# PSUM banks by name: a turn of eight outside a recurrent scan, a list of 258 inside it

## The chip, the cores and the metric

The kernel runs on one core of a Trainium2 chip. Five engines work side by side on their own queues: TensorE (PE, matmuls), VectorE (DVE), ScalarE (ACT), GpSimd (POOL), and SyncE (SP), which here issues the DMAs. Matmuls write to PSUM, an on-chip memory of eight banks of 128 partitions by 2 KB; the other engines read the results from there. The metric is the device time of one execution in microseconds, the median of the runs shown.

## What is computed

One layer of a hybrid diffusion block over 512 latent tokens and 256 context tokens of width 1024: a combined input projection feeds an RWKV-7 branch (token shift, a delta-rule scan in two directions over 16 heads of 64) and a gMLP branch; gates merge them, an output projection follows, and then an expert-choice mixture of 16 SwiGLU experts. Cut to what matters for the stages that the change touches:

```python
def centred_shift(z, w):
    zp = jnp.pad(z, ((0, 0), (1, 1), (0, 0)))
    return zp[:, :-2] * w[0] + zp[:, 1:-1] * w[1] + zp[:, 2:] * w[2]

def decay(dw, w0, w2):                                  # rwkv_prep, per direction
    w = -jax.nn.softplus(-(w0 + jnp.tanh(dw) @ w2)) - 0.5
    return jnp.exp(-jnp.exp(heads(w)))
a_f = jax.nn.sigmoid(p["a0"][0] + daf @ p["a2"][0])
kk = kk * lax.rsqrt(jnp.maximum(jnp.sum(kk * kk, -1, keepdims=True), 1e-12))

def step(S, inp):                                       # rwkv_scan
    r_t, k_t, v_t, d_t, kk_t, a_t = inp
    s_kk = jnp.einsum('bhvk,bhk->bhv', S, kk_t)
    S_new = (S * d_t[:, :, None, :] - s_kk[..., None] * (kk_t * a_t)[:, :, None, :]
             + v_t[..., None] * k_t[:, :, None, :])
    y = jnp.einsum('bhvk,bhk->bhv', S if reverse else S_new, r_t)
    return S_new, y

def token_mixer(h, p, s0_f, s0_b, n_chunks):
    z = h @ p["w_in"]
    ...
    merged = g_a * (y_a @ p["w_branch_a"]) + g_s * (y_s @ p["w_branch_b"])
    return merged @ p["w_out"], s_f, s_b
```

## The kernel before

The stages follow one another along the span: loads, the modulation and the transposed inputs (`ht`) up to about 60 us; the projection with its preparation of the scan in eight blocks of 128 channels up to about 330; the gMLP values `zv`, gates and spatial gating up to 575, with the first parts of the scan mixed in; the scan's chunk steps from 575 to 862; readout, branches and output projection up to about 1000; and the experts to the end.

Every matmul group writes one PSUM tile of 128 by 512 float32, a full bank. All 789 of them come from one call, `P` (L70), which takes them from a pool with a single tag and eight buffers (L54); the framework decides which buffer a tile gets when the one it takes is free again by its own model of the work. The program puts a semaphore wait in front of a tile's first matmul for the last reader of the tile that had the bank before. PE, ACT and SP run in the order in which the program is written (`manual_schedule`, L56); DVE and POOL too in the block loop and in the scan, where the code is again under `manual_schedule`.

In the block loop (L575 on), block `ct` does in written order: `z_k` (matmuls `zl` and `zc` over the latent and the context tokens), `prep_d1(ct-1)` (the reverse direction of the block before, nearly all of it on DVE), the shift of k (`shift_in`, L344: one ACT pass at L352, two DVE passes each for `zc` and `zl`, L354 and L356, into `kt`), `prep_v(ct-1)` (twelve transposes into four `vT` tiles, PE L513, read by ACT at L514), `prep_bonus(ct-1)` (`bon`), `prep_a(ct, 0)` (tiles `b2`, `b1`, `b1`; named `b` in the profile; the first matmuls go to the first `b1`), `prep_tanh` (four ACT passes, L427 and L428), the square of `kt` (ACT L402), `prep_scan` (DVE L436 and L438, ACT L440 to L445), `prep_kd` (DVE L449), `z_r` (`zl` and its shift into `rt`), `prep_k` (matmuls `b<-sq,bones`), work on DVE up to `prep_L`, then `z_v` and `prep_a(ct, 1)`. A block takes 18 PSUM tiles.

The scan runs 12 chunk steps of 64 tokens in two directions. Its order is a hand-written list of short words, `PLAN` (L1087) and `PLAN_END` (L1099), run by `run_plan` (L1115, called at L1376 to L1378): `K` transposes keys (`keys_t` L849, `bk`), `z`, `y`, `s` and `q` are the matmuls `zp`, `up`, `sp` and `qs` with what reads them (`zed` L862, `you` L871, `state` L880, `query` L897), `w` is the output `yp` (`why` L909), `a` the small products of a chunk (`prep` L679), `o` stores them for the triangular solve (`wave_out` L698, SP L704), `v`, `p`, `F` and `D` run the solve on DVE (`wave` L721, whose load of `Dt` is L723; rank-1 steps `tmpi` and `Xt` at L717 and L719), `i` loads its result (`wave_in` L744), and `V`, `X`, `S`, `U`, `R` and `l` are smaller steps and loads. So on each queue the order is fixed, and one late step holds what stands behind it.

Of the kernel before, what the change touches and what calls it, by code (L numbers as in the profile page):

```python
# [1 line left out]

# [5 lines left out]
F32 = mybir.dt.float32  # L8
# [35 lines left out]
def block_kernel(es: ExitStack, tc, x, ctx, cT, ada_w, ada_b, pc, rows, w_ch, w_vs, w2, a2, g2, sgu_w,  # L44
# [9 lines left out]
    pp = es.enter_context(tc.tile_pool(name="ps", bufs=8, space=PSUM))  # L54
# [5 lines left out]
    def nm(p):  # L60
        cnt[0] += 1
        return f"{p}{cnt[0]}"

    def T(shape, name="t", dt=F32):
        return big.tile(shape, dt, name=nm(name), tag="big", bufs=NBIG)

    def K(shape, name="t", dt=F32):
        return keep.tile(shape, dt, name=nm(name), tag="keep", bufs=NKEEP)

    def P(name="p"):  # L70
        return pp.tile([128, 512], F32, name=nm(name), tag="ps")

    def mm(o, l, r, start=True, stop=True):
        PE.matmul(o, l, r, start=start, stop=stop, skip_group_check=True)  # L74
# [144 lines left out]
    def ada_chunk(ws):  # L219
        p = P("ada")  # L220
        for k in range(KT):
            g = k % 4
            mm(p[32 * g:32 * g + 32, :], sP[:, k, :], ws[k // 2][:, k % 2, :], start=(k < 4), stop=(k >= 4))
        a = T([128, 512], "adao")
        S.activation(a, p, AF.Copy)
        return a
# [9 lines left out]
    def ada_cols(n):  # L236
        a = ada_chunk(aw.pop(n))
        p = P("adt")
        for b in range(4):
            PE.transpose(p[:, b * 128:b * 128 + 128], a[:, b * 128:b * 128 + 128], ident)  # L240
        which, b0 = divmod(n * 4, 8)
        dst = md[:, which, b0:b0 + 4, :]
        V.tensor_reduce(dst, p.rearrange("p (b g m) -> p b m g", b=4, g=4)[:, :, 0:2, :], AX.X, OP.add)
        V.tensor_tensor(dst, dst, adab_col[:, which, b0:b0 + 4, None].to_broadcast([128, 4, 2]), OP.add)
        if which == 1:
            V.tensor_scalar(dst, dst, 1.0, None, op0=OP.add)
# [23 lines left out]
    for d in range(2):  # L270
        for lst, src, nme in ((w2p, w2, "w2p"), (a2p, a2, "a2p")):
            t = T([128, D], nme)
# [7 lines left out]
    def hl(k):  # L280
        return hL[0][k // 2][:, k % 2, :], hL[1][k // 2][:, k % 2, :]

    def hc(k):
        return hC[0][k // 4][:, k % 4, :], hC[1][k // 4][:, k % 4, :]
# [23 lines left out]
    for k in range(KT):  # L308
        if k % 4 == 0:
            ada_cols(k // 4)  # L310
            ada_cols(k // 4 + 2)
            if k:
                zw.step()
        for (dst, i0, n, j) in ((hl(k), 2, 4, 0), (hc(k), 0, 2, 1)):
            p = P("ht")
            w = n * 128
            for i in range(n):
                PE.transpose(p[:, i * 128:i * 128 + 128], xts[i0 + i][:, k * 128:k * 128 + 128], ident)
            t = T([128, TL], "hf")
            V.tensor_scalar(t[:, :w], p[:, :w], md[:, 1, k, j:j + 1], md[:, 0, k, j:j + 1], op0=OP.mult, op1=OP.add)  # L320
            S.activation(dst[0], t[:, :w], AF.Copy)
            G.tensor_tensor(dst[1], t[:, :w], dst[0].bitcast(F32), OP.subtract)  # L322

    def zmm(w, want_ctx):
        wh, wl = (t.rearrange("p (k n) -> p k n", k=KT) for t in w)
        pl = P("zl")
        pc_ = P("zc") if want_ctx else None
        for k in range(KT):
            st, sp = k == 0, k == KT - 1
            hh, hlo = hl(k)  # L330
            mm(pl, wh[:, k, :], hh, st, False)
            mm(pl, wh[:, k, :], hlo, False, False)
            if want_ctx:
                ch_, cl = hc(k)
                mm(pc_[:, :TC], wh[:, k, :], ch_, st, False)
                mm(pc_[:, :TC], wh[:, k, :], cl, False, False)
                mm(pc_[:, :TC], wl[:, k, :], ch_, False, sp)
            mm(pl, wl[:, k, :], hh, False, sp)
        return pl, pc_
# [540 lines left out]
    def state(si, d):  # L880
        bk, sv, uv, svn = BK.pop((si, d)), SV[si, d], UV[si, d], SV[si + 1, d]
        u = uidx(si, d)
        sp = P("sp").rearrange("p (c n) -> p c n", c=KT)
        idt = (si, d) in IDENT
        if idt:
# [197 lines left out]
    for d in range(2):  # L1083
# [16 lines left out]
        "q10.1 p1 s9.1 U11 s9.0 w9 V10 h10.0 z10.1 X10 z10.0 p1 y10.1 h10.1 y10.0 p5 s10.1 R11 s10.0 p4 w10 p2 "  # L1100
        "i11 p1 z11.0 h10.2 p1 V11 p1 q11.1 X11 z11.1 h11.0 y11.0 q11.0 p3 y11.1 p2 h11.1 w11 h11.2 "
    ).split()
    IDENT = {(1, 0), (4, 0), (4, 1), (7, 1), (8, 0), (8, 1), (9, 1), (10, 1)}

    def finish_wave(w):
# [9 lines left out]
    def run_plan(plan, hook=None):  # L1115
        for t in plan:
            args = [int(a) for a in t[1:].split(".") if a]
            if t[0] == "h":
                hook(*args)
            elif t[0] == "t":  # L1120
                static_pair(1)
            else:
                OPS[t[0]](*args)
# [40 lines left out]
    def readout(half):  # L1164
        H = [K([128, 4, 256], "yAH", F32R) for _ in range(2)]
        L = [K([128, 4, 256], "yAL", F32R) for _ in range(2)]
        YA[half] = (H, L)
        for o, i in enumerate(HALF[half]):
            bo = GB[half][0][o]
            for b in range(2):  # L1170
                p = P("yT").rearrange("p (a n) -> p a n", a=4)
                pg = P("gg").rearrange("p (a n) -> p a n", a=4)
                t = T([128, 4, 128], "yf")
                for q in range(4):
                    ct = 4 * b + q
                    PE.transpose(p[:, q, :], yt[i][:, ct * 128:ct * 128 + 128], ident)
                    mm(pg[:, q, :], st_tp["g2"][:, ct * 128:ct * 128 + 128], sdg[:, i * 128:i * 128 + 128])
                for q in range(4):
                    ct = 4 * b + q
                    if b == 0:  # L1180
                        V.scalar_tensor_tensor(t[:, q, :], p[:, q, :], col("lnx_g", ct), bo[:, ct, :], op0=OP.mult, op1=OP.add)
                    else:
                        S.activation(t[:, q, :], p[:, q, :], AF.Copy, scale=col("lnx_g", ct))
                if b:
                    G.tensor_tensor(t, t, bo[:, 4 * b:4 * b + 4, :], OP.add)
                V.tensor_mul(t, t, pg)
                hd, ld = H[b][:, :, o * 128:o * 128 + 128], L[b][:, :, o * 128:o * 128 + 128]
                S.activation(hd, t, AF.Copy)
                V.tensor_tensor(ld, t, hd.bitcast(F32), OP.subtract)
# [43 lines left out]
    def out_mm(half, outs, mg, last=False):  # L1233
        ps = {(o, n): P("yx") for o in outs for n in range(2)}

        def term(q, k, w, ns):
            for o in outs:
                l = tuple(m[k // 4][:, k % 4, o * 128:o * 128 + 128] for m in mg)
                for n in ns:
                    cs = slice(n * 512, n * 512 + 512)  # L1240
                    mm3(ps[o, n], l, (w[0][:, cs], w[1][:, cs]), q == 0, q == KT - 1)

        for q, k in enumerate(range(KT) if half == 0 else KORD):
            if half == 0:
                w = aws.get(KT + k)
                if k in KRES:
                    wos[k] = w
            elif k in wos:
                w = wos[k]
                aws.fill()  # L1250
            else:
                w = wos[k] = aws.get(3 * KT - len(JRES) + KORD.index(k) - len(KRES))
            term(q, k, w, (0,) if last else (0, 1))
        if last:
            for q, k in enumerate(KORD):
                term(q, k, wos[k], (1,))
        return ps
# [101 lines left out]
    def early(si, at):  # L1359
# [8 lines left out]
        if si == nst - 1:  # L1368
# [4 lines left out]
            if at == 1:  # L1373
                readout(0)

    with tc.manual_schedule():  # L1376
        run_plan(PLAN)
    run_plan(PLAN_END, early)  # L1378
# [25 lines left out]
    ps = out_mm(0, (0, 1), MG.pop(0))  # L1404
# [7 lines left out]
    ps = out_mm(1, (0,), mg)  # L1412
    sid1 = out_ln(1, (0,), ps)
    next(sid1), next(sid1)
    ps = out_mm(1, (1,), mg, True)
# [36 lines left out]
    p = P("sT")  # L1452
# [233 lines left out]
```

## Time and profile before

| | us |
|---|---|
| median of 3 runs | 1976.82 (1973.1 to 1978.05) |
| the profiled execution | 1979.77 |
| its span, first to last instruction | 1978.0 |
| PE busy in the span | 1762.2 (89%) |
| DVE busy | 919.3 (46%) |
| ACT busy | 604.2 (31%) |
| mean granted TensorE clock | 0.967 of full speed |

The shares are means over stages with different limits, so they are to be read by stage: PE and DVE share the block loop, PE alone fills the stretch before the scan, chains of waits between PE, DVE and SP make the scan, and the experts' weights arriving by DMA set the pace at the end. Start times in the rows are microseconds from the span's start; a bracket at the end of a row is the time that the engine had been idle before it and what ended that.

### The profile page before, as it was taken

The numbers are of one execution on the slowest core, as the hardware profiler recorded it, in microseconds if no ns is written. First come the engines' busy times: TensorE is split into PE (matmuls) and PEld (weight loads), VectorE is DVE, ScalarE is ACT, GpSimd is POOL, SyncE is SP. The second block draws the span as 40 slices with busy tenths as digits, with TensorE's granted clock in tenths as the row PEclk, the third lists the DMA queues.
The fourth block names the chain that finished last, engine by engine and source line by source line (L and its number), as shares of the span: only waits on it lengthen the run. The fifth ranks groups of instructions, "written<-read, shape, count | busy, mean of one in ns | idle before, by whom it ended". The sixth has DMA issues, their size and how long they took to land.

```text
span 1978.0 us, 32483 instructions
## 1 busy us (share of the span) xinstructions
PE 1762.2 (89%) x13252; PEld 1122.8 (57%) x13252; DVE 919.3 (46%) x1685; ACT 604.2 (31%) x1058; POOL 239.2 (12%) x203
## 2 busy tenths in 40 slices
PE   6989999999987978788959999899998989899895
PEld 3877777878876867687844434334343323334324
DVE  6688886687837768786950020110102002020105
ACT  2666766233246645343221111101011101111101
POOL 4422234110110100055300000000000000000000
PEclk9999999999999989898969999999999999999998
DMA  9265657667697667584189999999999999999995
GB/s 331 92 194 155 188 155 238 193 225 228 237 261 160 154 146 179 114 266 138 65 348 427 426 428 426 426 427 427 426 427 427 427 427 426 427 427 427 427 418 201
DMA packets 363757, 590.34 MB, mean 298 GB/s; under 512 B 220372, under 2 KB 282324, under 8 KB 315480
## 3 DMA queue, kind: packets, MB, share of 16 engines
q1 hardware_dynamic: 363608, 588.26, 80.6%
q8 instruction: 105, 1.72, 0.3%
q14 instruction: 44, 0.36, 0.1%
HBM read 539.69 MB, written 47.71 MB: 297 GB/s over the span
## 4 chain that ended last, share of the span: by engine, by line
DMA 44%; PE 26%; DVE 11%; issue 3%; SPq 2%; ACT 1%; POOL 0%; DVEq 0%; ACTq 0%; POOLq 0%
DMA we<-in_e 42%; PE zl L74 5%; PE hh L74 3%; PE zv L74 2%; PE sc L74 2%; DVE tmpi L717 2%; PE bb L74 2%; DVE Xt L719 2%; PE yx L74 2%; PE qs L74 2%; PE yp L74 1%; PE sp L74 1%; PE zp L74 1%; PE l L74 1%; PE up L74 1%
## 5 line engine op out<-in xcount | busy, mean ns | idle before, releaser
L74 PE MATMUL hh<-we,xe 128*64 128x512 f32 x2048 | 463.1, 597 | 24.5 <-DMA we<-in_e 24.2
L74 PEld LDWEIGHTS hh<-we,xe 128*64 128x64 f32 x2048 | 148.9, 137 | 324.6 <-issue 267.1
L74 PE MATMUL ye<-we,hidT 128*64 128x512 f32 (+1 forms) x1216 | 254.7, 533 | 37.8 <-DMA we<-in_e 37.5
L1521 DVE TENSOR_TENSOR hd<-hd,hh 64x512 f32<-64x512 f32 x64 | 44.1, 690 | 519.1 <-ACT hd L1520 518.7
L74 PE MATMUL zl<-hL,H 128*128 128x512 f32 x816 | 259.6, 400 | 1.9 <-DVE hf L320 1.2
L74 PEld LDWEIGHTS ye<-we,hidT 128*64 128x64 f32 x1216 | 83.3, 136 | 201.3 <-DMA we<-in_e 106.0
L1520 ACT ACTIVATE hd<-hh 64x512 f32<-64x512 f32 x64 | 37.9, 592 | 491.6 <-PE hh L74 491.6
L74 PEld LDWEIGHTS zl<-hL,H 128*128 128x128 f32 x816 | 153.9, 191 | 30.6 <-issue 2.6
L160 POOL TENSOR_TENSOR L<-w,H 128x1024 fp32r<-128x1024 f32 x54 | 138.4, 2571 | 236.6 <-ACT H L159 197.5
L74 PE MATMUL zl<-hL,L 128*128 128x512 f32 x408 | 162.1, 397 | 2.5 <-DVE L L160 2.5
L1614 POOL TENSOR_TENSOR x<-x,row 128x1024 f32<-128x1024 f32 x2 | 4.6, 2340 | 989.3 <-DVE rv L129 989.3
L159 ACT ACTIVATE H<-w 128x1024 fp32r<-128x1024 f32 x91 | 95.0, 1054 | 88.5 <-DMA w<-in_w_ch 36.1
L1539 ACT ACTIVATE ye<-ye 64x512 f32<-64x512 f32 (+1 forms) x34 | 18.9, 555 | 272.8 <-PE ye L74 272.5
L1540 DVE SCALAR_TENSOR_TENSOR ye<-ye,gate,srow 64x512 f32<-64x512 f32 (+1 forms) x38 | 23.9, 663 | 149.1 <-ACT ye L1539 148.8
L74 PEld LDWEIGHTS zl<-hL,L 128*128 128x128 f32 x408 | 78.1, 191 | 14.4 <-DVE L L160 3.6
L717 DVE TENSOR_TENSOR tmpi<-Dt,Xt 128x31 f32<-128x31 f32 (+15 forms) x186 | 63.6, 342 | 18.0 <-DMA Dt<-Asd 12.5
L719 DVE TENSOR_TENSOR Xt<-Xt,tmpi 128x31 f32<-128x31 f32 (+15 forms) x186 | 63.8, 343 | 6.4
L74 PEld LDWEIGHTS xe<-oh,h 128*128 128x128 f32 x512 | 59.6, 196 | 8.9 <-issue 8.9
L74 PE MATMUL co<-ye,ohT 128*128 128x512 f32 (+1 forms) x144 | 62.7, 591 | 0.0
L74 PE MATMUL xe<-oh,h 128*128 128x128 f32 x512 | 61.8, 282 | 0.7 <-DVE oh L1470 0.7
L74 PEld LDWEIGHTS zc<-hC,H 128*128 128x128 f32 x288 | 54.0, 188 | 12.7 <-POOL hC L322 0.4
L1496 DVE COPY gate<-gate 64x1 f32<-64x1 f32 x16 | 2.5, 156 | 122.7 <-PE gate L74 122.4
(332 smaller groups left out, 2908.8 us busy)
## 6 DMA issues: line engine op xcount, KB each, us to landing
we<-in_e SPq DMA_DIRECT2D x376, 1024.0 KB, 19.6
w<-in_w_ch SPq DMA_DIRECT2D x51, 512.0 KB, 5.0
w<-in_ada_w SPq DMA_DIRECT2D x32, 512.0 KB, 5.6
xx<-Xkd SPq DMA_DIRECT2D x28, 512.0 KB, 5.6
adaw<-in_ada_w SPq DMA_DIRECT2D x16, 512.0 KB, 10.3
we<-in_e SPq DMA_DIRECT2D x32, 256.0 KB, 5.4
Xkd<-g SPq DMA_DIRECT2D x32, 192.0 KB, 2.7
Ald<-al SPq DMA_DIRECT2D x16, 384.0 KB, 2.3
```

Source lines behind the costliest of these rows:

```text
L74: PE.matmul(o, l, r, start=start, stop=stop, skip_group_check=True)
L159: S.activation(h, t, AF.Copy)
L160: (eng or G).tensor_tensor(l, t, h.bitcast(F32), OP.subtract)
L717: V.tensor_tensor(tv, Dt[:, j, None, j + 1:].to_broadcast([128, m, n]), X[:, 0:m, j:j + 1].to_broadcast([128, m, n]), OP.mult)
L719: V.tensor_tensor(X[:, 0:m, j + 1:], X[:, 0:m, j + 1:], tv, OP.subtract)
L1496: V.tensor_copy(g[j * 64:j * 64 + 64], p[j * 64:j * 64 + 64, j:j + 1])
L1520: S.activation(hd, pn[n][0:64], AF.Silu)
L1521: V.tensor_tensor(hd, hd, pn[n][64:128], OP.mult)
L1539: S.activation(y, p, AF.Copy)
L1540: V.scalar_tensor_tensor(y, p if same else y, gv[e - j][rs], gt2[rs, cs], op0=OP.mult, op1=OP.mult)
L1614: G.tensor_tensor(acc[i], acc[i], l2[0], OP.mult)
```

## The change

`P` now names the bank. Each bank becomes a tag of its own, `ps0` to `ps7`, with one buffer. Outside the scan the bank is the next in turn after the last, and a bank is passed over while Python still holds a reference to its tile. Before the scan's plan runs, a list `order` is filled with 258 digits, `BANKS`, and each call of `P` takes the next of them until the list is empty; by the count of tiles it covers all of `PLAN` and `PLAN_END` up to the readout. No instruction of any engine is added or taken away, and the written order stays. A `del p, t` behind the loop of the transposed inputs lets go of its last tile.

```diff
+import sys
...
+    banks, nextb, order = {}, [0], []
+
     def P(name="p"):
-        return pp.tile([128, 512], F32, name=nm(name), tag="ps")
+        if order:
+            b = order.pop(0)
+        else:
+            b = next((x % 8 for x in range(nextb[0], nextb[0] + 8)
+                      if x % 8 not in banks or sys.getrefcount(banks[x % 8]) <= 2), nextb[0] % 8)
+            nextb[0] = b + 1
+        banks.pop(b, None)
+        banks[b] = t = pp.tile([128, 512], F32, name=nm(name), tag=f"ps{b}", bufs=1)
+        return t
...
+    del p, t
...
+    BANKS = (
+        "0123456701234567012345670123456701235647012356041235670412356704123670415243672041536720415376240153"
+        "7624015376240153762401624501632745016327415603274156302756413027564132064715320647153210536247103562"
+        "4710356245671034256714256714250367142560731425607314256073"
+    )
...
+    order += [int(b) for b in BANKS]
     with tc.manual_schedule():
         run_plan(PLAN)
     run_plan(PLAN_END, early)
```

## Rows read from the trace of the kernel before

**Rows 1.** Busy by stretch: from:to, length, PE PEld DVE ACT POOL, PEclk, DMA share, GB/s
```profile
125.00:325.00 200.00, 184.30 (x963) 153.25 (x962) 176.20 (x195) 138.90 (x213) 56.41 (x34) 0.98 0.57 174
...
370.00:575.00 205.00, 200.85 (x970) 165.34 (x968) 158.77 (x268) 66.71 (x105) 14.96 (x23) 1.00 0.68 222
...
1030.00:1960.00 930.00, 864.60 (x4252) 357.02 (x4248) 126.31 (x237) 103.40 (x200) 0.00 (x0) 0.99 1.00 420
```

**Rows 2.** PE's waits, 70 to 340 us: us in total, times, longest
```profile
PE b L74 <- ACT vs L514: 19.0, 7, 3.3
```

**Rows 3.** Timeline of PE, block 2: start, duration, instruction
```profile
135.78 0.79 PE L74 MATMUL b<-xp,wp 128*128 128x512 f32 x1
...
138.48 0.50 PE L74 MATMUL b<-xc,wp 128*128 128x256 f32 x2 [1.69 <-ACT vs L514]
...
145.02 1.45 PE L74 MATMUL b<-sq,bones 128*128 128x512 f32 x4
```

**Rows 4.** Timeline of DVE, blocks 2 and 3
```profile
143.01 0.75 DVE L356 SCALAR_TENSOR_TENSOR kt<-zl,pcol,kt 128x511 f32<-128x511 f32 x1
...
150.12 0.75 DVE L354 SCALAR_TENSOR_TENSOR rt<-zl,pcol,rt 128x511 f32<-128x511 f32 x1 [2.64 <-ACT rt L352]
...
175.11 0.75 DVE L356 SCALAR_TENSOR_TENSOR kt<-zl,pcol,kt 128x511 f32<-128x511 f32 x1
```

**Rows 5.** Timeline of ACT, block 2
```profile
139.32 0.73 ACT L427 ACTIVATE g<-b,pcol 128x512 f32<-128x512 f32 x1
...
140.82 0.54 ACT L428 ACTIVATE a<-b,pcol 128x256 f32<-128x256 f32 x1
143.86 0.94 ACT L402 ACTIVATE sq<-kt,pcol 128x768 f32<-128x768 f32 x1 [2.51 <-DVE kt L356]
...
146.72 0.85 ACT L443 ACTIVATE Ge<-L 128x768 f32<-128x768 f32 x1 [0.99 <-DVE L L438]
...
149.41 0.67 ACT L352 ACTIVATE rt<-zl,pcol 128x512 f32<-128x512 f32 x1
```

**Rows 6.** Busy time by stretch, behind three waits of PE; PEclk is the third from last
```profile
170.00:174.00 4.00, 3.42 (x17) 2.92 (x18) 3.93 (x4) 3.45 (x9) 1.75 (x2) 1.00 0.33 123
...
202.00:206.00 4.00, 3.38 (x11) 2.83 (x12) 3.93 (x4) 3.60 (x9) 1.79 (x2) 0.65 0.33 125
...
640.40:644.00 3.60, 3.56 (x22) 3.42 (x24) 0.62 (x1) 1.89 (x4) 0.00 (x0) 0.57 0.47 160
```

**Rows 7.** PE's waits in the scan, 575 to 862 us
```profile
PE bk L856 <- DVE qs L907: 10.8, 1, 10.8
PE yp L74 <- DVE sv L894: 10.4, 1, 10.4
PE bk L856 <- DVE sv L894: 9.0, 1, 9.0
```

**Rows 8.** DVE's waits in the scan, 637 to 862 us
```profile
DVE sv L894 <- PE sp L74: 10.1, 4, 5.2
DVE tmpi L717 <- DMA Dt<-Asd: 9.3, 3, 5.3
DVE qs L907 <- PE qs L74: 9.1, 4, 5.1
DVE al L695 <- ACT ap L692: 6.8, 1, 6.8
```

**Rows 9.** Timeline of PE, 8 us behind the first of the three waits
```profile
648.64 1.15 PE L74 MATMUL zp<-sv,al 128*64 128x64 f32 x32
```

**Rows 10.** Timeline of DVE, the `sv` that this `zp` reads
```profile
640.33 0.69 DVE L895 TENSOR_TENSOR sv<-sv,gC 64x512 f32<-64x512 f32 x1
```

**Rows 11.** Timeline of SP's queue from chunk 6 on
```profile
707.96 2.52 SPq L755 DMA_DIRECT2D tp<-Xsd  x4
715.02 1.90 SPq L704 DMA_DIRECT2D Asd<-ap  x4
...
733.89 0.56 SPq L723 DMA_DIRECT2D Dt<-Asd  x1
```

## The prediction, made blind

> **What bounds the kernel now.** The busy table by stage comes first [rows 1]: it says where a microsecond of TensorE (PE) counts. From 125 to 325 us, the eight blocks of the projection loop, PE is busy for 184.3 of 200 us and VectorE (DVE) for 176.2: the two hand the bound to each other. From 370 to 575 PE alone is the bound, 200.85 of 205, so a delay that reaches 370 is carried on. From 1030 on the DMA share is 1.00 and the experts' weights set the time; that stage only starts earlier or later. Between 575 and 862 lies the scan. For an edit of PSUM banks the second view is PE's waits in these stretches [rows 2, 7]. A matmul that stands waiting for an engine that does not make its operands waits for its bank. There are two families: `b` waiting for ScalarE's (ACT) copies of `vT`, 19.0 us in seven, and in the scan `yp` and twice `bk` waiting for DVE, 30.2 us in three. The third view is the order of work, read as timelines, to see what each wait pushes [rows 3 to 6, 9 to 11].
>
> **The turn of eight, outside the scan.** No instruction is added or removed; only who waits for whom changes. A block takes its tiles in this order: `zl`, `zc` of k (0, 1), four `vT` (2 to 5), `bon` (6), `b2` and two `b1` of `prep_a` (7 to 9), `zl` of r (10), then eight more, 18 in all. A strict turn puts tile 8, the bank of `prep_a`'s first matmuls, on that of tile 0. Python no longer holds tile 0 there, so nothing makes the turn skip it. Its last reader is DVE's second shift of `kt` (L356), which stands on DVE behind the whole `prep_d1` of the block before. In block 2, PE is at these matmuls at 135.78 [rows 3], and that shift ends at 143.01 + 0.75 = 143.76, called K [rows 4]. PE would wait 7.98 us, where today it waits 1.69 one matmul later, for `vs`. Behind it on PE's queue stand the other `b`, all of `z_r`, and `prep_k`'s sums; ACT's four Tanh and DVE's `rt` wait for those.
>
> What it costs. Today `z_r` ends at 145.02. From K on PE has 145.02 - 138.48 = 6.54 us of work plus the first pair of `b`, which I put at 0.5 (the pair at 138.48, of half the width, has 0.50): 7.04 at full clock. PE's clock falls after such waits: after the 9.0 us one in the scan the granted clock was 0.57 for 3.6 us, and 0.65 for 4 us behind one of today's `b` waits, of 3.3 us at most [rows 2, 6], so (1 - 0.65) x 4 = 1.4 to (1 - 0.57) x 3.6 = 1.55 us are lost. `z_r` then ends at K + 8.6; ACT's copy takes 0.67 [rows 5], and DVE's `rt` starts at about K + 9.4, with a tenth for hand-overs. Today it starts at 150.12 = K + 6.36, having waited 2.64 for that copy [rows 4]. So a block gets 9.4 - 6.36 = 3.0, say 3.1, longer. If the clock stayed up, ACT would be as late as PE: 0.6 for the first `b`, 141.36 - 139.32 = 2.04 of Tanh, then 150.08 - 143.86 = 6.22 less the 0.99 that it waited [rows 5], is K + 7.9, and a block loses 1.5. Block follows block at 175.11 - 143.01 = 32.10 us, and the six periods from block 1 to block 7 lose 6 x 3.1 = 18.6. Behind the last K no DVE work is the bound any more: there PE's own delay counts, K + 8.6 against 145.02 = K + 1.26, which is 7.3. **Sum of this part: 18.6 + 7.3 = 25.9, say +26** (bounds: 6 x 1.5 + 5.8 = 15, and 28 with hand-overs of two tenths more per block). The 19.0 us of today's waits are no gain, as they lie in the time that PE now spends waiting for K.
>
> Elsewhere outside the scan I put the turn at nothing: from 370 to 575 every tile eight places back is read out within the next tile's matmuls, and PE's 4.15 us of idle leave no room to win. Without that cover one wait there would cost its length, some tenths to 2 us; the range holds that.
>
> [...]
>
> **The list, in the scan.** BANKS gives each tile a bank by position, with at least four tiles between two uses. The waits of `bk` (9.0), `yp` (10.4) and `bk` (10.8) [rows 7] are on banks whose reader is far back on DVE; I take them to go. What is late next decides. (a) After the first, PE could go on 9.0 us earlier, but `zp` at 648.64 [rows 9] needs DVE's `sv`, which ends at 640.33 + 0.69 = 641.02 [rows 10]: the shift is 648.64 - 641.02 = 7.6, less a hand-over, 7.5. DVE had waited for PE there, so it keeps the shift. (b) After the second, PE could be up to 7.5 + 10.4 = 18 us early, but SyncE (SP), which issues loads and stores in written order, is not: today its `tp` loads end at 707.96 + 2.52 = 710.48, it then waits until 715.02 for ACT's `ap`, and issues back to back to the load of `Dt` at 733.89, for which DVE stands waiting [rows 8, 11]. With loads 7.5 earlier and no wait for `ap`, the stores start at 703.0, 12.0 earlier, and so does `Dt`. (c) After the third, DVE's waits for `qs` (9.1, the longest 5.1 [rows 8]) could go; most of the loads of the last chunks then come late, and I take 5. **Sum: 12 + 5 = 17 gained.** Bounds: 7.5, say 8, if (a) alone is kept; and 10.1 + 9.3 + 9.1 + 6.8 = 35, all that DVE waits there [rows 8].
>
> **Net** 26 - 17 = +9 us. The profiled execution took 1979.77 us, 1.77 over its span of 1978.0, and would take 1988.8; it lies 2.95 over the median of the runs, 1976.82, so the median goes to 1985.8.
>
> **The rivals.**
> 1. *The clock stays up in the blocks.* Behind block 3's `b` wait the granted clock was 1.00 [rows 6], and the waits shrink: PE has 7.04 + 22.86 (145.02 to 135.78 + 32.10) = 29.9 us of work from one K to the next wait, so in a period of 33.6 to 35.2 it waits some 4 to 5 us, no longer 8. Then 15 - 17 = -2: 1975. Against it: behind block 4's it was 0.65 [rows 6].
> 2. *The other side: SP is not the limit in the scan.* Place: SP's queue from 707.96 to 733.89. Price: up to the 35 us that DVE waits. Point: whether `Dt` lands before DVE has finished chunk 6's `sv`. If it does, 26 - 35 = -9: 1968. Against it: 18.9 us of issues from 715.02 to 733.89 lie back to back [rows 11].
> 3. *The turn does not put `b` on `zl`'s bank*, since something still holds that tile, so that the skip takes a bank of `vT` as today: 0 - 17, 1960. For it: the skip looks at references only. Against it: `z_k` pops its tiles out of `st_` before `prep_a`.
> [...]
> 5. *The list gives nothing*, because its model of the order is not what the chip does (a `qs` tile four places behind a `bk` waits for ACT instead): +26, 2003.
>
> **How the numbers follow.** The forecast has 0.57, the rivals 0.14, 0.07, 0.07, 0.03 and 0.12. The predicted time is 1986. About 0.3%, 5.9 us, is what a measurement can tell from no change. Of the forecast's 0.57 I give 0.10 to net changes under 5.9 (a loss near 20, a gain near 17) and 0.47 to slower; rival 1 is same, 5 slower, 2 to 4 faster. Faster 0.17, same 0.24, slower 0.59. The range is 1966 to 2003: it takes in rivals 1 and 2, the high bound 28 - 8 = +20 (1997), and half of rival 5; left out are 3, 4 and the other half, 0.16. Forecast's own range: 1978 to 1997.
>
> **What would show it.** In PE's waits from 70 to 340, a row `b` waiting for DVE's `kt` (L356), seven times, 4 to 10 us each, in place of `vs`; DVE's `rt` waiting 5 to 6 us per block instead of 2.64; the start of the `kt` shift from one block to the next at 35 us instead of 32.10; the granted clock low behind those waits. In the scan, the three long waits gone, DVE's `sv` after 641 no longer waiting for PE, SP's `Dt` load some 12 us earlier against the scan's start. It would be wrong if `b` still waits for `vs` (rival 3), if the period grows by only 1.5 (rival 1), or if SP's row shows gaps and `Dt` comes 17 us early (rival 2).

## The result and the profile after

| | before | after |
|---|---|---|
| median, us (4 runs each) | 1977.43 (1973.1 to 1978.93) | 1991.87 (1987.57 to 1993.89) |
| ratio, 95% interval | | 1.0078 (1.0055 to 1.0102) |
| profiled execution, us | 1979.77 | 1993.89 |
| its span, us | 1978.0 | 1991.0 |

The change makes the kernel 14.4 us slower. The forecast was 1986, +9.

No instruction was added, so each stands in both traces in the same place of its queue, and its start in the one can be taken from its start in the other. The shift along the kernel shows where the time went (us; a positive shift is later than before):

| point | before | after | shift |
|---|---|---|---|
| K (end of `kt`'s last shift on DVE), block 1 | 111.65 | 109.92 | -1.7 |
| K, block 7 | 304.00 | 321.88 | +17.9 |
| PE's first `cs`, behind the blocks | 368.6 | 393.9 | +25.3 |
| DVE `al`, early in the scan | 591.40 | 618.37 | +27.0 |
| DVE `qs`, behind the first long wait | 654.92 | 675.98 | +21.1 |
| DVE `tmpi` | 676.15 | 698.44 | +22.3 |
| DVE `qs`, behind the second | 777.58 | 794.18 | +16.6 |
| DVE `sv`, behind the third | 826.34 | 837.06 | +10.7 |
| PE's first `yT` of the readout | 860.8 | 873.9 | +13.1 |
| PE's first `lg`, router | 988.0 | 1005.0 | +17.0 |
| PE's first `hh`, experts | 1028.5 | 1044.0 | +15.5 |

27 us are lost in front of the scan, 16 are won in it, and 5 to 6 are lost again behind it.

**The blocks.** PE's waits from 60 to 350 us (us in total, times, longest). The row for `vs` [rows 2] is gone; this stands in its place:

```profile
PE b L85 <- DVE kt L369: 37.1, 7, 9.2
```

Timelines of the changed kernel in block 2: PE, DVE and ACT (start, duration, instruction, idle before and what ended it), to be held against [rows 3 to 5]:

```profile
145.92 0.47 PE L85 MATMUL b<-xp,wp 128*128 128x512 f32 x1 [4.31 <-DVE kt L369]
...
154.42 1.45 PE L85 MATMUL b<-sq,bones 128*128 128x512 f32 x4
```

```profile
145.03 0.75 DVE L369 SCALAR_TENSOR_TENSOR kt<-zl,pcol,kt 128x511 f32<-128x511 f32 x1
...
148.61 0.56 DVE L449 TENSOR_SCALAR g<-g 128x768 f32<-128x768 f32 x1 [2.24 <-ACT g L441]
...
155.34 0.75 DVE L367 SCALAR_TENSOR_TENSOR rt<-zl,pcol,rt 128x511 f32<-128x511 f32 x1 [3.08 <-ACT rt L365]
...
179.65 0.75 DVE L369 SCALAR_TENSOR_TENSOR kt<-zl,pcol,kt 128x511 f32<-128x511 f32 x1
```

```profile
146.66 0.69 ACT L440 ACTIVATE g<-b,pcol 128x512 f32<-128x512 f32 x1 [4.83 <-PE b L85]
...
154.62 0.69 ACT L365 ACTIVATE rt<-zl,pcol 128x512 f32<-128x512 f32 x1 [0.67 <-PE zl L85]
```

K is 145.03 + 0.75 = 145.78; PE's `b` starts 0.14 us behind it, `z_r` ends at 154.42 = K + 8.64, and `rt` starts at K + 9.56. The next K is 34.62 later, where it was 32.1. ACT's first Tanh waits 4.83 us for `b`, and DVE's `g` now waits for the Tanh.

Busy time by stretch behind three of these waits (columns as in [rows 1]; PEclk is third from last):

```profile
145.90:150.00 4.10, 4.08 (x13) 3.34 (x14) 1.83 (x3) 2.58 (x5) 0.00 (x0) 0.61 1.15 332
180.50:184.50 4.00, 3.95 (x12) 3.32 (x13) 1.30 (x3) 2.03 (x5) 0.00 (x0) 0.57 1.13 333
...
322.00:326.00 4.00, 3.97 (x11) 3.33 (x12) 1.01 (x2) 1.72 (x4) 0.00 (x0) 0.50 1.14 330
```

Microsecond by microsecond, the granted clock behind the first of them was 0.95 from 145.90, 0.50 from 146.90 to 149.90, 0.84 from there and 1.00 from 150.90; behind the second it was 0.50 from 181.50 to 183.50; in the third stretch it was 0.50 throughout.

**The scan.** PE's waits from 600 to 880 us. The three long ones of [rows 7] are not there; the longest that are left:

```profile
PE zp L85 <- DVE sv L908: 6.6, 7, 2.1
PE sc L85 <- DMA xx<-Xkd: 5.0, 1, 5.0
PE yT L1194 <- DVE qs L920: 4.4, 1, 4.4
```

DVE's waits from 655 to 880 us, against [rows 8]:

```profile
DVE tmpi L730 <- DMA Dt<-Asd: 10.5, 3, 6.5
DVE L L171 <- ACT H L170: 6.9, 1, 6.9
DVE sv L907 <- PE sp L85: 6.7, 4, 5.2
...
DVE al L708 <- ACT ap L705: 2.6, 3, 1.8
...
DVE qs L920 <- PE qs L85: 1.9, 3, 1.4
```

Most of the waits for `qs` and `al` and part of those for `sv` went; the one for `Dt`'s load stayed.

**The start of the readout.** SP, ACT, DVE and PE:

```profile
865.19 2.60 SPq L183 DMA_DIRECT2D w<-in_wba  x4
```

```profile
870.75 1.06 ACT L170 ACTIVATE H<-w 128x1024 fp32r<-128x1024 f32 x1 [4.17 <-DMA w<-in_wba]
```

```profile
871.84 1.23 DVE L171 TENSOR_TENSOR L<-w,H 128x1024 fp32r<-128x1024 f32 x1 [6.86 <-ACT H L170]
```

```profile
873.88 0.44 PE L1194 MATMUL yT<-ident,y 128*128 128x128 f32 x1 [4.42 <-DVE qs L920]
```

The turn, which goes on with bank 0 behind the list, puts the readout's first `yT` on the bank of one of the scan's last `qs`. Its reader on DVE stands behind `L<-w,H`, which waits for ACT's `H`, which waits for a load that SP issues late. Before, `yT` followed the last `up` at once (860.79).

### The profile page after: what moved, and what is told of

It is laid out like the page before. It is cut to its first block, busy times and chain, and to the rows that moved or that the text cites. A ratio compares the mean times of both kernels' runs of the same rounds, so it can differ in the third digit from the quotient of the medians.

```text
span 1991.0 us, 32426 instructions
## 1 busy us (share of the span) xinstructions
PE 1768.2 (89%) x13252; PEld 1131.3 (57%) x13252; DVE 917.9 (46%) x1685; ACT 603.9 (30%) x1058; POOL 233.6 (12%) x203
## 4 chain that ended last, share of the span: by engine, by line
DMA 41%; PE 8%; DVE 5%; issue 1%; POOL 0%; ACT 0%; DVEq 0%; SPq 0%; POOLq 0%
DMA we<-in_e 41%; PE hh L85 3%; PE yx L85 2%; PE ye L85 1%; PE co L85 1%; PE xe L85 0%; PE lg L85 0%; DVE mt L1232 0%; DVE x L1290 0%; DVE mgL L1236 0%; DVE wk L1466 0%; DVE m L1465 0%; PE h2T L1336 0%; DVE mt L1231 0%; PE ba L85 0%
## 5 line engine op out<-in xcount | busy, mean ns | idle before, releaser
L1539 ACT ACTIVATE hd<-hh 64x512 f32<-64x512 f32 x64 | 37.9, 592 | 490.7 <-PE hh L85 490.7
L171 POOL TENSOR_TENSOR L<-w,H 128x1024 fp32r<-128x1024 f32 x54 | 133.7, 2483 | 273.5 <-ACT H L170 253.5
L85 PEld LDWEIGHTS zl<-hL,L 128*128 128x128 f32 x408 | 78.6, 193 | 14.7 <-DVE L L171 3.6
L171 DVE TENSOR_TENSOR L<-w,H 128x1024 fp32r<-128x1024 f32 x37 | 45.6, 1236 | 30.2 <-ACT H L170 23.0
## 6 DMA issues: line engine op xcount, KB each, us to landing
we<-in_e SPq DMA_DIRECT2D x376, 1024.0 KB, 19.6
```

What stands on the lines that cost most here:

```text
L171: (eng or G).tensor_tensor(l, t, h.bitcast(F32), OP.subtract)
L1539: S.activation(hd, pn[n][0:64], AF.Silu)
```

## Experiments

Ratios are against runs of the kernel before on the same chip (its medians there: 1978.77 for e0 to e3, 1977.68 for e4 to e7, 1977.35 for e8 to e10 and 1974.81 for e11).

| kernel | median, us | ratio, 95% interval |
|---|---|---|
| e0_named | 1978.02 | 1.0000 (0.9976 to 1.0023) |
| e1_hold | 1961.60 | 0.9914 (0.9887 to 0.9941) |
| e2_turn_only | 2005.45 | 1.0141 (1.0121 to 1.0161) |
| e3_list_only | 1961.81 | 0.9921 (0.9904 to 0.9938) |
| e4_fill | 1981.76 | 1.0031 (1.0007 to 1.0056) |
| e5_w_first | 1989.55 | 1.0054 (1.0036 to 1.0073) |
| e6_no_b_wait | 1973.25 | 0.9970 (0.9954 to 0.9985) |
| e7_hold_w_first | 1956.92 | 0.9890 (0.9873 to 0.9907) |
| e8_w_later | 1966.08 | 0.9959 (0.9940 to 0.9978) |
| e9_all | 1959.02 | 0.9914 (0.9887 to 0.9942) |
| e10_later | 1952.77 | 0.9879 (0.9852 to 0.9905) |
| e11_tail | 1984.44 | 1.0060 (1.0035 to 1.0085) |

**Naming alone (e0).** Every tile gets by name the bank that it had before.

```diff
-    banks, nextb, order = {}, [0], []
+    ALL = (...)                    # 789 digits: the banks of the kernel before
+    banks, nextb, order = {}, [0], [int(b) for b in ALL]
...
-    order += [int(b) for b in BANKS]
```

> All 789 tiles get by name the bank that the framework had picked in the kernel before (read from the program before, up to a renumbering of the banks). My theory, that nothing but the order of reuse of the banks matters: 1977, the same waits of `b` for `vs` and of `bk` and `yp` for DVE as before. Rival, that eight tags of one buffer cost something of their own (other SBUF slots, other semaphores): slower by up to the 14 us of the change.

1978.0, no difference, with a block period of 32.05. So what follows is due to which bank is used when, and not to the eight tags.

**The two halves apart (e2, e3).** In e2 the digits of `BANKS` are replaced by the banks that the kernel before used there, and 284 more digits keep the reuse that the changed kernel's turn has behind the scan; e3 has the banks of before everywhere and the list only in the scan.

> The turn of eight outside the scan, as in the changed kernel, and in the scan the banks of the kernel before. My theory, that the list brings some 12 us net and the turn costs 26: 1977 + 26 = 2003, with the three waits of `bk` and `yp` of 9 to 11 us back. Rival, that the turn alone makes the difference and the list nothing: 1992.

> The banks of the kernel before outside the scan, and in it the list of the change. My theory: blocks as before (period 32.1), the three long waits in the scan gone, and a part of that given back in the readout: 1977 - 12 = 1965. If the whole of my forecast for the list (17) holds: 1960. Rival, that the list gains only because the loss ahead of the scan had shifted the phase of the loads: 1977.

e2: 2005.5, +26.7. e3: 1961.8, -17.0. PE's waits of e2 in the scan and of e3 in the blocks and the scan:

```profile
PE bk L869 <- DVE qs L920: 10.8, 1, 10.8
PE yp L85 <- DVE sv L907: 10.6, 1, 10.6
PE bk L869 <- DVE sv L907: 9.1, 1, 9.1
```

```profile
PE b L95 <- ACT vs L537: 20.0, 7, 3.5
```

```profile
PE zp L95 <- DVE sv L918: 5.7, 6, 2.0
```

Each half has its own waits, as forecast. The rivals fall: neither half is nothing. The halves add up to 9.7, where the change has 14.4; the intervals are wide enough for that. The list gained more (17) than the 12 that I expected from the changed kernel's trace; a loss of that size behind the scan is what e11 finds.

**One bank in the blocks (e1).** Two lines make the turn pass over the k tiles until the block's Tanh are written.

```diff
             st_[ct] = {"ps": zmm(zw.get(3 + 3 * ct), True)}
+            st_[ct]["hold"] = st_[ct]["ps"]
...
             prep_tanh(ct, 0)
+            st_[ct].pop("hold")
```

> The changed kernel, with the k tiles `zl` and `zc` of a block kept referenced until the four Tanh of that block are written, so that the turn passes their two banks over and `prep_a` takes the banks of `vT` again. My theory, that in the blocks the one bank of `zl` is the whole loss: the waits of `b` for `kt` go, the period of a block is 32.1 again, and 25 to 27 us of the 14.4 lost come back: 1992 - 26 = 1966, about 11 below the kernel before. Rival, that the turn costs by other waits too (or that the list gains nothing): 1977 or above.

1961.6: 30 us below the changed kernel, from passing over two banks in each block. `b` waits for `vs` again (13.2 us in four). This is more than the 26 expected: the periods are 29.9 and 32.1 in turn, so that PE's first `cs` starts 6.1 us ahead of the kernel before. That came as a surprise and led to e8.

**The clock's part (e4).** 16 matmuls of no use fill PE's wait.

```diff
         p2 = P("b2")
+        for _ in range(16 if ct and d == 0 else 0):
+            mm(p2, w2p[0][:, cs], dwt[0][0][0])
```

> The changed kernel with 16 added matmuls of 512 columns per block (into the `b2` tile, which is overwritten afterwards), placed where PE stands waiting for `kt` for 4.3 us, so that PE is busy during the wait and its clock stays up; they are worth 16 x 0.24 = 3.8 us. It parts what the low clock costs from what the wait costs. Theory (the low clock is about half of the 3.3 us that a block is longer): the period falls from 35.3 to about 33.7, and with the last block 6 x 1.6 + 1.5 = 11 come off 1992: 1981. Rival (the chain over the Tanh, the reverse sum on DVE and ACT's exponentials sets the period at any clock): 1990 to 1992.

1981.8. PE in block 2, and the clock behind the wait:

```profile
142.07 4.21 PE L85 MATMUL b<-xp,wp 128*128 128x512 f32 x16
147.03 0.47 PE L85 MATMUL b<-xp,wp 128*128 128x512 f32 x1 [0.74 <-DVE kt L369]
```

```profile
145.00:149.00 4.00, 3.26 (x17) 2.48 (x16) 2.44 (x4) 1.00 (x2) 0.00 (x0) 1.00 1.07 274
```

PE still has to stay until K, but the clock is 1.00, `rt` starts at K + 8.25 instead of 9.55, and the period is 33.17 in the middle blocks against 34.6. So some 10 of the 27 us that the blocks lose are what the lower clock behind the waits costs (0.50 to 0.67 over 4 us in the changed kernel), and the rest is the wait. By my estimate it is rather more than 10: the longest wait that the added work left was 5.6 us, and in the changed kernel even waits of 4.3 us had 0.50 to 0.67 over 4 us behind them. Doing 4.2 us of useless work per block made the kernel faster.

**SP's order in the readout (e5, e7).** The weight loads stand ahead of the readout's.

```diff
-                readout_load(0)
                 aws.load_to(3)
+                readout_load(0)
```

> The changed kernel with one step moved: the weight loads of the first output projection (`w`) are written ahead of the readout's ten loads (`bo`, `gb`) on SP's queue instead of behind them. Theory (SP's queue, back to back from 837.8 to 865.2 us, brings `w` so late that ACT and DVE wait 4.2 and 6.9 us at the readout's start, and PE's first `yT` 4.4 behind them): 4 us less, 1988. Rival (the readout is late for another reason, the transfers themselves): no change, 1992.

> The kernel that keeps the k tiles referenced (1961.6) together with the weight loads written first. Theory of the SP queue: another 4 less, 1957 to 1958. Rival: 1962.

SP issues `w` from 851.07 on, ACT's `H` no longer waits there, and PE's first `yT` starts at 868.86 without a wait. The medians are 2.3 lower on the changed kernel and 4.7 lower on e1. Both lie within the intervals, and the trace of e5 gives most of the start's gain back: from the last `sv<-sp,sv` of DVE to the first `hh` it takes 187.2 us, the changed kernel 188.2. So SP's late `w` is the end of that chain of waits, but not shown to be the loss.

**Behind the scan (e11).** The list is longer: the tiles from the readout on have the banks of before, too.

```diff
     BANKS = (
         ...
+        ...                        # 284 digits: the banks of before behind the scan, renumbered
     )
```

> The changed kernel, with the tiles behind the scan (readout, branches, output projection, experts) on the banks of the kernel before instead of in turn; the blocks and the scan stay as changed. From the last `sv` of the scan to the first `hh` of the experts the kernel before takes 183.4 us, the changed one 188.2. Theory (the turn behind the scan costs by itself, by the wait of the first `yT` and between the output projection and the router): 184 to 185 there, and 1992 - 3.5 = 1988. Rival (the 4.8 us are what the loads on SP's queue give back whatever the banks): 188 there, 1992.

1984.4 (1988 expected), 9.6 above before on its chip, where the change stood 14.4 above. The intervals of the two ratios overlap, so the traces have to decide. From the last `sv<-sp,sv` to the first `hh` it takes 179.5 us (before 183.3, changed 188.2). Of the 8.7 us against the changed kernel 4.5 lie ahead of the first `yT` (13.5 against 18.0) and 2.5 between the output projection's first `yx` and the router's `lg` (70.9 against 73.4). PE's waits from 840 to 1046 us; the row of `yT` for DVE's `qs` is not among them:

```profile
PE sT L1476 <- DVE wk L1472: 14.7, 1, 14.7
PE aT L1361 <- DVE aff L1359: 2.4, 2, 1.6
PE ba L85 <- DVE L L171: 2.3, 1, 2.3
```

SP's order is the same as in the changed kernel. The turn behind the scan costs by itself; the rival falls. The other traces bear this out: the stretch from `sv` to `hh` takes 179.5 to 183.7 us in the six kernels with the banks of before there and 184.5 to 188.6 in the eight with the turn, and its part from `yx` to `lg` 70.6 to 71.2 against 72.6 to 74.9. The part ahead of `yT` does not set the two apart (13.4 to 15.7 against 13.2 to 18.0); its wait for `qs` comes back in e4 alone.

There the turn is not one of eight: it passes over the four `yx` tiles that the program still holds, so the `ba` and `yx` behind them go round four banks, where the kernel before used eight. Whether this makes the 2.5 us was not tested.

**The `b` waits of before (e6, e8).** The forecast said that the 19.0 us in which `b` waits for `vs` today are no gain. e6 takes them off `b` with three `vT` tiles for four and `bon` behind `prep_a`:

```diff
+        pm = P("vT")
         for d, src in enumerate((s["v"], s.pop("vr"))):
             vs = T([128, 6, 128], "vs")
-            for lo, n in ((0, 4), (4, 2)):
-                p = P("vT")
+            for lo, n, p, o in ((0, 4, P("vT"), 0), (4, 2, pm, 256 * d)):
...
-                prep_bonus(ct - 1)
-                flush()
             prep_a(ct, 0)
+            if ct:
+                prep_bonus(ct - 1)
+                flush()
```

> The kernel before with the waits of `b` for `vs` mostly taken away by other means: the transposes of v take three PSUM tiles instead of four (the two halves of 256 share one), and `bon` comes behind `prep_a`, so that all of `b` finds a free bank. Theory (these 19 us of waits lie in time that PE has anyway, the block's period is set by DVE and ACT): the period stays near 32.1 and the time within 3 us of before, 1977. [...]

1973.3, 4.4 less: far from the 19.0 of those waits, but not nothing either. The period fell to 29.88 in the middle blocks. PE now waits elsewhere, 14.7 us in all, so e6 took only some 4 us of waiting away and does not show by itself what all 19.0 are worth:

```profile
PE vT L513 <- ACT vs L514: 14.7, 8, 5.2
```

The shorter period has another cause. It does not go by the length of `b`'s wait: in the kernel before that is 1.7 us in some blocks and 3.2 to 3.3 in others, and the middle periods are 32.0 to 32.1 in both. What differs is seen in e1, inside one kernel. DVE and POOL in two of its blocks:

```profile
126.05 0.95 DVE L502 SCALAR_TENSOR_TENSOR L<-L,a 128x768 f32<-128x768 f32 x1
...
155.95 3.16 DVE L502 SCALAR_TENSOR_TENSOR L<-L,a 128x768 f32<-128x768 f32 x1
```

```profile
126.34 2.94 POOL L171 TENSOR_TENSOR L<-w,H 128x1024 fp32r<-128x1024 f32 x1 [6.75 <-ACT H L170]
...
155.09 3.21 POOL L171 TENSOR_TENSOR L<-w,H 128x1024 fp32r<-128x1024 f32 x1 [5.59 <-ACT H L170]
```

The same DVE operation takes 0.95 us when it starts ahead of POOL's and 3.16 when POOL's came first: it then ends 0.8 us behind POOL's, nearly its own length. The difference, 2.2, is that between the two periods. e8 moves POOL's operation and ACT's `H` ahead of it, and names no bank:

```diff
             z_v(ct)
-            zw.step()
-            if ct > KT - 3:
-                zw.step()
             prep_a(ct, 1)
             prep_tanh(ct, 1)
+            zw.step()
+            if ct > KT - 3:
+                zw.step()
```

> The kernel before with one step moved in each block: the split of the next weights behind `z_v` (ACT's copy `H`, then POOL's `L`) is written behind `prep_a` and the four Tanh instead of ahead of them, so that POOL's 2.4 us operation starts some 2 us later and no longer at the same time as DVE's `L<-L,a`. No bank is named. Theory (a block is 32.1 us when DVE's `L<-L,a` meets POOL and takes 3.16, and 29.9 when it does not and takes 0.95; behind the blocks PE is the bound and keeps only some 5 of it): period near 29.9, and 1978 - 5 = 1973, although all waits of `b` for `vs` stay. Rival (the shorter blocks of the two kernels that showed 29.9 came from fewer waits of `b`): period 32.1, 1978.

Median 1966.1, and the periods are 29.94 to 30.03 in the middle blocks. Its DVE and POOL:

```profile
153.45 0.95 DVE L488 SCALAR_TENSOR_TENSOR L<-L,a 128x768 f32<-128x768 f32 x1
```

```profile
154.53 2.40 POOL L160 TENSOR_TENSOR L<-w,H 128x1024 fp32r<-128x1024 f32 x1 [7.54 <-DVE L L488]
```

`b` still waits seven times for `vs`, 10.7 us in all, and the period is as short as in e6. Here the framework picks the banks, and with the step moved it picked others for four tiles of each block, so e8 alone leaves the banks as a rival. e10, below, does the same move on e7 with every tile on the bank that it has there: e7's periods are 29.8 to 29.9 and 32.1 in turn, e10's are 30.0 in the four middle blocks, and in its one longer block (31.4) POOL meets `g`, 2.08 us instead of 0.73. ACT's `H` stands in the same place in both kinds of e1's blocks. So the collision sets it. I had expected that PE would keep all but 5 us; the gain came to 11 by the medians (8 by the ratio), so PE was not the bound behind the blocks to that extent.

**Together (e9, e10).** e9 is e7 with e6's edits in the blocks, e10 is e7 with e8's.

> The turn with the k tiles kept referenced, the list, the weights first, and the transposes of v in three tiles with `bon` behind `prep_a`. Theory: blocks of 29.9 throughout, the list's 17 and the SP queue's 4: 1953 to 1956, at or a little below the 1957 of the best so far, since PE is the bound behind the blocks. Rival (the gains add up in full): 1978 - 4 - 17 - 5 = 1952 or less.

> The turn with the k tiles kept referenced, the list, the weights first, and the split of the next weights behind the Tanh in each block. Theory: where the blocks now alternate between 29.9 and 32.1 all become 29.9, of which PE's work keeps 2 at most: 1955. Rival: POOL's operation meets another of DVE's, 1957 to 1960.

e9: 1959.0, above what I expected, so e6's arrangement adds nothing to e7. e10: 1952.8 (1955 expected), the fastest of all, 24.6 below before and 39 below the change; it is the change with the k tiles kept referenced, and two steps reordered. Its blocks still hold another such meeting. DVE's `g<-L,kd` in the kernel before, where it once started ahead of POOL, and in e10, with POOL's operation:

```profile
297.65 0.95 DVE L473 TENSOR_TENSOR g<-L,kd 128x768 f32<-128x768 f32 x1
```

```profile
164.48 3.12 DVE L487 TENSOR_TENSOR g<-L,kd 128x768 f32<-128x768 f32 x1
```

```profile
164.33 2.46 POOL L171 TENSOR_TENSOR L<-w,H 128x1024 fp32r<-128x1024 f32 x1 [5.21 <-ACT H L170]
```

No run moved this one, so what it costs a block is open.

## Why the prediction was nearly right, step by step

- *Where `b` waits, and for what.* Right: seven waits for `kt` in place of `vs`, on the bank of `zl`. The first is 9.2 us; of the later ones all but the last (6.3) are 4.3 to 4.4, as rival 1's working said (4 to 5).
- *The chain from K to `rt`.* K + 9.4 forecast; K + 9.53 to 9.56 in four of the blocks, K + 10.6 to 10.8 in the first and the last two. In those three PE is late by more than I had: `z_r` ends at K + 9.7 to 9.9 instead of 8.6, and ACT stands waiting for it. ACT's copy for `rt` in block 6, and the 6 us behind PE's wait there:

```profile
294.10 0.69 ACT L365 ACTIVATE rt<-zl,pcol 128x512 f32<-128x512 f32 x1 [1.18 <-PE zl L85]
```

```profile
284.10:290.10 6.00, 5.95 (x16) 4.92 (x17) 2.82 (x3) 3.71 (x6) 0.00 (x0) 0.50 1.01 288
```

  In blocks 4 and 5 ACT is the late one: `z_r` is there at K + 8.6 and 8.4, but ACT is busy until K + 8.9 with what follows its Tanh. I had priced that chain at full clock only.
- *The clock.* It fell behind every wait (0.50 to 0.67 over 4 us), so rival 1 is out, although its shorter waits came. e4 prices it for the kernel at 10 us. For PE alone I had 1.4 to 1.55 us a block; against e4, where `z_r` ends at K + 7.1 at full clock, it is 1.3 to 1.6 in four blocks and 2.6 to 2.8 in three.
- *The waits of DVE.* This sign was missed: `rt` waits 2.3 to 3.6 us, not 5 to 6, because DVE now stands waiting ahead of `g` too (2.24 us in block 2).
- *The period.* +3.1 forecast, 35.33 - 32.06 = +3.27 on average. The six periods run from 34.4 to 37.9, and the agreement of the mean is partly luck. It hides two more terms, which DVE's timelines of the kernel before and then of the changed one show for block 2:

```profile
158.45 3.15 DVE L488 SCALAR_TENSOR_TENSOR L<-L,a 128x768 f32<-128x768 f32 x1
...
163.88 0.55 DVE L436 TENSOR_SCALAR g<-g 128x768 f32<-128x768 f32 x1
```

```profile
163.67 0.95 DVE L501 SCALAR_TENSOR_TENSOR L<-L,a 128x768 f32<-128x768 f32 x1
...
167.05 1.98 DVE L449 TENSOR_SCALAR g<-g 128x768 f32<-128x768 f32 x1
```

  POOL's operation no longer meets `L<-L,a` (-2.2), but `g` behind it (+1.4). In the last period (37.88) POOL also meets `L<-rmask,g`, 3.84 us instead of 1.76. Against the block of 29.9, in which `L<-L,a` meets nothing, a block of the changed kernel is over 5 us longer.
- *The sum of the blocks.* 25.9 forecast; 19.6 + 7.4 = 27.0 in the trace, 26.7 in e2, which has the turn behind the scan too, so that its blocks come to less. The 7.4 behind the last K against my 7.3 is luck: `z_r` ends there at K + 9.7 where I had 8.6, and ended before at K + 2.3 where I had taken block 2's 1.26. The upper bound, 28, is 27.3 by its own words (25.9 + 7 x 0.2).
- *The list.* 17 forecast; 17.0 in e3, and 16.3 in the changed kernel (+27.0 to +10.7). Its parts were 5.9, 4.5 and 5.9, where I had 7.5, 4.5 and 5; so the load of `Dt` came 10 us earlier against the scan's start, not 12, and the total was met better than its parts. (In four places the list has three tiles between two uses of a bank, not four.)
- *The step that failed: "elsewhere outside the scan I put the turn at nothing".* I had argued that for the stretch from 370 to 575 and said nothing of the stages behind the scan. There the turn costs the changed kernel about 5 us (14.4 to 9.6 by the medians of the change and of e11, each against its own before; 183.3 to 188.2 in the traces). With that taken out, e11 stands 9.6 above before, close to my 26 - 17. So the mechanism and both large terms held, and a term of about 5 was left out; the range, not the sum, covered it.
- *The 19.0 us of waits.* That they would go as a gain, to which 0.03 was given (rival 4), no run shows. In the blocks a plain turn made 37.1 us of waits out of 19.0; e6 had 14.7 of them on `vT` and gained 4.4. In the scan, banks in an order other than a plain turn brought 17 us.

## What to carry to other kernels

Here a PSUM bank was written again only when its last reader had run, and that was far down another engine's queue (`b` waited 9.2 us for DVE's `kt` in block 1): before banks are taken in turn, look for the tile with the late reader, and let the turn pass it over. PE's stalls of 4.3 to 9.2 us cost the wait and then some 2 to 6 us at a granted clock of 0.50 (249.80 to 251.80 in block 5, 284.10 to 290.10 in block 6), so price both. Walk the whole kernel with a rule that applies to the whole kernel: the term that was missed lay in the stage that was not looked at.

## What the runs showed of the hardware that was not expected

An operation of DVE over 128x768 float32 took 0.95 us alone (`L<-L,a` at 129.06 in the changed kernel) and 3.00 to 3.17 us when POOL's `TENSOR_TENSOR` over 128x1024 had started up to 0.9 us earlier (in the kernel before 3.16 at 126.33, 3.00 at 298.64); when DVE started first, POOL took 2.85 us (e6) and 2.94 (e1) instead of 2.41. Other DVE operations beside a running POOL operation, the shifts that read PSUM, kept their 0.48 and 0.74 us (e6, e8). `g<-g`, which reads one tile where `L<-L,a` reads two, was held up too (1.98 us instead of 0.55). Why POOL and DVE hold each other up, and which operations do, was not shown: no run changed an operation's inputs. A shift of a few tenths of a microsecond on one engine moved the block's period by 2.2 us: in block 1 POOL started 0.07 us ahead of `L<-L,a` in the kernel before (126.26 and 126.33), and that took 3.16; in e1 it started 0.29 behind (126.34 and 126.05), and that took 0.95. So a change elsewhere can seem to gain or lose by it.
